# Two of three chunks of the last gate by way of DRAM, and the output projection two softmax steps sooner

## The chip, the cores and the metric

The kernel runs on one core of one Trainium2 chip. The metric is device time in microseconds (us), the median of several executions. TensorE (PE) multiplies, VectorE (DVE) and ScalarE (ACT) do elementwise work, GpSimd (POOL) does some too and issues DMAs, and SyncE (SP) only issues DMAs. The engines run side by side, each in a fixed order of instructions, and wait for one another by semaphores. A scheduler fixes each engine's order when the program is built.

## What is computed

Two layers of an encoder on 16 + 1024 = 1040 positions of width 1024, in float32. Each layer has a gated linear attention (GLA, 4 heads), a softmax attention with a forget-gate bias (FoX, 8 heads of 64), an output projection of both with a residual add, and a convolutional MLP. The part that matters here:

```python
xn = rms_norm(h, attn_norm[i])
gq, gk, gv, gr, glr, fq, fk, fv, ff = jnp.split(xn @ w_in[i], cuts, axis=-1)
...
o_gla = rms_norm(o_gla, gla_norm[i].reshape(GLA_HEADS, GLA_DV)).reshape(B, L, GLA_WIDTH)
o_gla = o_gla * jax.nn.silu(gr)
...
o_fox = forgetting_attention(fq.reshape(B, L, FOX_HEADS, FOX_DH),
                             fk.reshape(B, L, FOX_HEADS, FOX_DH),
                             fv.reshape(B, L, FOX_HEADS, FOX_DH), log_f).astype(h.dtype)
o_fox = rms_norm(o_fox, fox_norm[i].reshape(FOX_HEADS, FOX_DH)).reshape(B, L, FOX_WIDTH)
h = h + jnp.concatenate([o_gla, o_fox], axis=-1) @ w_out[i]
```

`silu(gr)`, with `gr` = four column blocks of 128 of the input projection, is "the gate" below: gate h belongs to GLA head h.

## The kernel before

Activations stand transposed: 128 features on the partitions, positions along the free axis, so a 1040-wide row is one of KD = 8 tiles. Float32 products are made of three fast matmuls (`mm3`, L249 to L255): each operand is split into a high and a low part (on ACT L378 the high, on DVE L379 the low), and the products high x high (L253), low-weight x high (L254) and high-weight x low (L255) are added up in PSUM.

The attention half of a layer is one function, `fox()` (L844). It walks through 72 softmax steps: 4 pairs of FoX heads with 18 steps each, a step being one head and one tile of 116 rows. A step has score matmuls on PE (L740, L741), a masked score with its maximum on DVE (L748), the exponential on ACT, transposes (L777) whose results DVE and ACT split (`PT`), and products with V (L795); a fold at the end of a row group (L808 to L842) brings the normalised head output, which is stored to DRAM (`mixd`). The last pair begins at step 54.

Between those matmuls PE gets filler: units of dense matmuls from a queue (`Work`, L131). One unit (`unit`, L262) is one chunk of columns of one 128-feature output tile: K matmul triples (8 for an input projection, 7 here for the output projection) and an evacuation. The list `starts` says at which steps the queue is emptied and refilled by `plan(p)`; within a stretch the units are spread evenly over its steps. Before, `starts` = 4, 22, 40, 58, 62, 80:

- from step 40, `plan(2)`: the products q, k, v of the last pair (9 units) and gate 2 (3 units)
- from step 58, `plan(3)`: gate 3 (3 units, chunks of 348, 348 and 344 columns, from the right), and the loads of `land[0]`, `[1]`, `[2]`, `[4]`, `[5]`, the GLA and FoX outputs that wait in DRAM (`mixd`)
- from step 62, `plan(4)`: the first four tiles of the output projection (12 units of 256, 384 and 400 columns, from the right)

`land` are the seven tiles from which the output projection is made; their order in each unit is `KORD` = 4, 5, 0, 1, 2, 3, 6. `land[3]` is gate 3's tile: the evacuation in `gr_products` (L685) writes there directly, while gates 0, 1 and 2 write to a scratch tile `gx` and from there to `mixd` in DRAM (L708, a DMA on POOL). One chunk of a gate has six operations on DVE (L693, L696, L700, then L703, L704, L706 behind the next step's scores, `later`) and three on ACT (L697 to L699). The slots of `land` are those of the second last pair, so they are free from step 58.

The first unit of the output projection carries a `feed` (L1040 to L1051): the splits of the seven land tiles, at most a few ahead of each matmul triple, and the residual loads.

## Time and profile before

| | |
|---|---|
| three runs | 2507.65, 2507.73, 2510.3 us |
| profiled execution | 2508.94 us, its span 2507.2 |
| mean granted clock of TensorE | 0.998 of full speed |
| instructions | 48346 |
| DMA traffic | 258.25 MB, 103 GB/s on average |

A span is the time from the first to the last instruction of one profiled execution. A row of the timeline reads: start, duration, engine, line, operation, output and inputs by name, size, and in brackets how long the engine had been idle and who released it. Windows give each engine's busy time in a stretch with its count, the clock granted to PE and the share of the DMA engines. Waits are totals, counts and the longest. Matmuls are pipelined: one that takes 0.32 by its own may start 0.16 after the one before it, so costs are read from start to start.

### The profile page before, as it was taken

The page shows a single profiled execution, that of the slowest core. Times are in us where ns is not written, and L with a number is a line of the kernel's source. Part 1 is how long each engine was busy: PE and PEld are TensorE (multiplying, and loading weights), DVE is VectorE, ACT ScalarE, POOL GpSimd, SP SyncE. Part 2 cuts the span into 40 slices and gives each one's busy share as a digit, 9 for nine tenths or more (in the row PEclk, how much of TensorE's full clock was granted, in tenths as well). Part 3 has the DMA queues.
Part 4 walks back from the last instruction along what each step waited for, and adds up shares of the span by engine and source line. Part 5 has one row for each costly group of instructions (what it writes and reads, how often), then busy time and mean ns, then how long its engine had stood idle before and what let it go on. Part 6 is the DMA issues. An engine that isn't in the chain of part 4 may idle for free.

```text
span 2507.2 us, 48346 instructions
## 1 busy us (share of the span) xinstructions
PE 2457.3 (98%) x19282; PEld 2410.2 (96%) x19282; DVE 1718.2 (69%) x3287; ACT 1272.3 (51%) x2548; POOL 403.2 (16%) x578
## 2 busy tenths in 40 slices
PE   8999999999999999999999999999999999999998
PEld 7999999899999999999999999998999999999997
DVE  7655676769877777853565666776797777787445
ACT  7345666556444445631343565674564444455312
POOL 4033433110000000100210334331100000001002
PEclk9999999999999999999999999999999999999999
DMA  3232134342322224763312233153332222257622
GB/s 123 71 89 75 54 88 129 111 149 72 115 81 81 77 77 139 198 170 110 105 54 70 75 86 87 44 164 109 127 96 98 76 81 81 78 165 177 199 60 78
DMA packets 115955, 258.25 MB, mean 103 GB/s; under 512 B 14496, under 2 KB 31040, under 8 KB 115728
## 3 DMA queue, kind: packets, MB, share of 16 engines
q1 hardware_dynamic: 92832, 181.74, 23.3%
q0 software_dynamic: 22176, 72.68, 10.3%
q8 instruction: 151, 2.47, 0.4%
q10 hardware_dynamic: 720, 0.74, 0.1%
q14 instruction: 76, 0.62, 0.1%
HBM read 174.50 MB, written 67.81 MB: 97 GB/s over the span
## 4 chain that ended last, share of the span: by engine, by line
PE 65%; issue 16%; DVE 10%; DMA 4%; ACT 4%; POOL 1%; SPq 0%; DVEq 0%; POOLq 0%; ACTq 0%
PE mm L253 7%; PE mm L255 7%; PE mm L254 7%; PE up L253 6%; PE up L255 6%; PE up L254 6%; PE down L253 5%; PE down L255 5%; PE down L254 5%; PE av L795 3%; PE tr L777 2%; PE wo L253 1%; PE wo L255 1%; PE wo L254 1%; DVE P L748 1%
## 5 line engine op out<-in xcount | busy, mean ns | idle before, releaser
L253 PE MATMUL up<-x,hi 128*128 128x260 f32 (+1 forms) x2464 | 697.2, 283 | 2.2 <-DVE hg L1322 1.4
L255 PE MATMUL up<-x,hi 128*128 128x260 f32 (+1 forms) x2464 | 695.4, 282 | 2.4 <-DVE x L1144 2.4
L254 PE MATMUL up<-x,lo 128*128 128x260 f32 (+1 forms) x2464 | 696.1, 283 | 0.0
L255 PEld LDWEIGHTS up<-x,hi 128*128 128x128 f32 x2464 | 465.7, 189 | 3.3 <-DVE x L1144 3.3
L253 PEld LDWEIGHTS up<-x,hi 128*128 128x128 f32 x2464 | 464.7, 189 | 3.1 <-DVE hg L1322 1.8
L254 PEld LDWEIGHTS up<-x,lo 128*128 128x128 f32 x2464 | 464.9, 189 | 0.1
L1120 DVE TENSOR_TENSOR lo<-raw,hi 128x512 fp32r<-128x512 f32 x364 | 247.9, 685 | 184.7 <-ACT hi L1119 177.0
L253 PE MATMUL mm<-xh,hi 128*128 128x348 f32 (+4 forms) x1056 | 360.5, 341 | 0.0
L255 PE MATMUL mm<-xl,hi 128*128 128x348 f32 (+4 forms) x1056 | 339.2, 321 | 0.0
L254 PE MATMUL mm<-xh,lo 128*128 128x348 f32 (+4 forms) x1056 | 338.3, 320 | 0.0
L1119 ACT CAST hi<-raw 128x512 fp32r<-128x512 f32 x364 | 224.5, 620 | 146.5 <-PE up L255 84.4
L253 PEld LDWEIGHTS mm<-xh,hi 128*128 128x128 f32 x1056 | 199.6, 189 | 3.0 <-issue 2.1
L254 PEld LDWEIGHTS mm<-xh,lo 128*128 128x128 f32 x1056 | 199.5, 189 | 0.3
L254 PE MATMUL down<-ah,lo 128*128 128x260 f32 (+1 forms) x704 | 198.1, 281 | 0.4 <-DVE lo L222 0.4
L255 PE MATMUL down<-al,hi 128*128 128x260 f32 (+1 forms) x704 | 198.4, 282 | 0.0
L255 PEld LDWEIGHTS mm<-xl,hi 128*128 128x128 f32 x1056 | 198.3, 188 | 0.0
L253 PE MATMUL down<-ah,hi 128*128 128x260 f32 (+1 forms) x704 | 197.9, 281 | 0.0
L379 DVE TENSOR_TENSOR PT<-tr,PT 116x464 fp32r<-116x464 f32 (+3 forms) x240 | 122.6, 515 | 70.3 <-ACT PT L378 68.4
L220 ACT CAST hi<-raw 128x512 fp32r<-128x512 f32 (+1 forms) x160 | 96.8, 607 | 122.3 <-PE down L255 96.0
L756 ACT ACTIVATE P<-P,m 116x924 f32<-116x924 f32 (+4 forms) x144 | 110.5, 768 | 73.0 <-DVE m L748 70.1
L1347 POOL DMA_DIRECT2D actd<-cv x44 | 23.5, 535 | 763.9 <-DVE cv L1346 758.0
L777 PE MATMUL tr<-ident,P 116*116 116x116 f32 x704 | 143.2, 266 | 2.5 <-DVE PT L379 1.3
(303 smaller groups left out, 5733.0 us busy)
## 6 DMA issues: line engine op xcount, KB each, us to landing
raw<-in_wm_dram SPq DMA_DIRECT2D x322, 256.0 KB, 2.8
raw<-in_wd_dram SPq DMA_DIRECT2D x64, 256.0 KB, 4.0
actd<-cv POOLq DMA_DIRECT2D x22, 520.0 KB, 2.9
actd<-cv POOLq DMA_DIRECT2D x22, 512.0 KB, 3.0
cb<-cd SPq DMA_DIRECT2D x16, 520.0 KB, 4.0
st<-actd SPq DMA_DIRECT2D x14, 520.0 KB, 4.7
st<-actd SPq DMA_DIRECT2D x14, 512.0 KB, 4.6
kA<-kA SPq DMA_DIRECT2D x24, 260.0 KB, 4.2
```

Source lines behind the costliest of these rows:

```text
L220: nc.scalar.copy(hi[:, :n, :], raw[:, :n, :])
L253: nc.tensor.matmul(ps, wh, xh[:, c0:c0 + n], start=first, stop=False, skip_group_check=more)
L254: nc.tensor.matmul(ps, wl, xh[:, c0:c0 + n], start=False, stop=False, skip_group_check=more)
L255: nc.tensor.matmul(ps, wh, xl[:, c0:c0 + n], start=False, stop=last, skip_group_check=more)
L379: nc.vector.tensor_tensor(out=lo, in0=src, in1=hi.bitcast(F32), op=ALU.subtract)
L748: self.scored = nc.vector.tensor_tensor_reduce(out=x, in0=S[:rows, :n], in1=cb[:rows, c0:k1], scale=1.0, scalar=(BIG if ci == 0 else m[:ro ...
L756: nc.scalar.activation(x, x, AF.Exp, scale=-1.0, bias=low, accum_out=(den if nch < 3 else d2[:rows, 0:1]))
L777: nc.tensor.transpose(tr[:w, j, :rows], P[:rows, o:o + w], id_)
L795: nc.tensor.matmul(av[:, a:width], w.rearrange("p a b -> p (a b)"), x, start=(t == 0 and i == 0), stop=(t == last and i == 1))
L1119: nc.scalar.copy(hi[:, :nk, :], src[:, :nk, :])
L1120: nc.vector.tensor_tensor(out=lo[:, :nk, :], in0=src[:, :nk, :], in1=hi[:, :nk, :].bitcast(F32), op=ALU.subtract)
L1347: nc.gpsimd.dma_start(self.actd[j][:, o0:T], uo)
```

## The change

`gr_products` gets a choice of chunks and of weights. Gate 3's chunks 2 and 1 (columns 692 to 1040 and 344 to 692) join `plan(2)`, that is, 14 units instead of 12 from step 40 to 58; they are stored to `mixd[3]` and read back in one DMA once gate 3's last chunk has been issued (`later`). `plan(3)` keeps chunk 0 alone (344 columns), with the weights that chunks 2 and 1 have loaded, and still writes to `land[3]`. `starts` gets 60 in place of 62. The other land tiles are loaded in two pieces each: columns 784 to 1040 on SP, the first 784 on POOL; `land[2]` is no longer held back.

```diff
--- before.py
+++ after.py
@@ -682,7 +682,7 @@
     def fox_free(self, q):
         self.slots.put(*q["qA"], *q["kA"], *q["kL"], *q["V"])

-    def gr_products(self, lyr, h, work, ap, pp, nm, dst=None):
+    def gr_products(self, lyr, h, work, ap, pp, nm, dst=None, chunks=CH_FOX, w=None):
         nc = self.nc

         def ev(ps, c0, n):
@@ -711,7 +711,7 @@
                 with self.tc.issue_after(self.scored.ins):
                     refine()
             self.later.append(behind)
-        self.add_tile(work, pp, self.wm[lyr, M_GR + h], nm["x"], CH_FOX if dst is None else CH_FOX[::-1], ev)
+        self.add_tile(work, pp, self.wm[lyr, M_GR + h], nm["x"], chunks, ev, w=w)


     @staticmethod
@@ -850,7 +850,7 @@
         steps = [(p, g, e, ti) for p in range(4) for g in range(5) for e in range(2)
                  for ti in reversed(range(len(groups[g])))]
         first = [steps.index((p, 0, 0, 1)) for p in range(4)]
-        starts = [f + 4 for f in first] + [first[3] + 8, len(steps) + 8]
+        starts = [f + 4 for f in first] + [first[3] + 6, len(steps) + 8]
         cbs, state, due = {}, {}, {}
         work, p_next = plan(-1), 0

@@ -1022,12 +1022,18 @@
                     if p < 3:
                         self.fox_products(lyr, p + 1, w, ap, pp, nm, qs[p + 1])
                         self.gr_products(lyr, p, w, ap, pp, nm)
+                        if p == 2:
+                            self.gr_products(lyr, 3, w, ap, pp, nm, chunks=CH_FOX[:0:-1])
+                            box["gate"] = w.boxes[-1]
                     elif p == 3:
                         land = box["land"] = [s.get(F32, f"h{k}") for k in range(KD - 1)]
-                        for k in (4, 5, 0, 1):
-                            nc.gpsimd.dma_start(land[k][:, :T], self.mixd[k][:])
-                        self.later.append(lambda: nc.gpsimd.dma_start(land[2][:, :T], self.mixd[2][:]))
-                        self.gr_products(lyr, 3, w, ap, pp, nm, land[3])
+                        c2, c3 = CH[2][0], CH_FOX[0][1]
+                        for k in (4, 5, 0, 1, 2):
+                            nc.sync.dma_start(land[k][:, c2:T], self.mixd[k][:, c2:T])
+                        for k in (4, 5, 0, 1, 2):
+                            nc.gpsimd.dma_start(land[k][:, :c2], self.mixd[k][:, :c2])
+                        self.later.append(lambda: nc.gpsimd.dma_start(land[3][:, c3:T], self.mixd[3][:, c3:T]))
+                        self.gr_products(lyr, 3, w, ap, pp, nm, land[3], CH_FOX[:1], box["gate"]["w"])
                     elif p == 4:
                         land = box["land"]
                         for c0, n in reversed(CH):
```

Where instructions move is shown at three places, all in layer 0.

VectorE up to the low split of gate 3's tile for the projection's first unit (`ml3` of 128x256); `ml4`, `ml5`, `ml6` are the same for the other tiles, `P` and `PT` belong to the softmax, and `P_6041` and `P_6038` are the first scores behind it. Before:

```order
L379 TENSOR_TENSOR ml5_5999<-h5_5668,mh5_5998 128x256
L693 TENSOR_TENSOR gx_5977<-mm_5899,r_149 128x344
L818 TENSOR_REDUCE fv_5943<-fo_5934 116x4
L696 TENSOR_SCALAR ge_5976<-gx_5977 128x344
L700 TENSOR_TENSOR gog_5974<-gx_5977,gog_5974 128x344
L222 TENSOR_TENSOR lo_6056<-raw_6053,hi_6055 128x512
L222 TENSOR_TENSOR lo_6062<-raw_6059,hi_6061 128x512
L379 TENSOR_TENSOR ml2_5993<-h2_5665,mh2_5992 128x256
L379 TENSOR_TENSOR ml3_5995<-h3_5666,mh3_5994 128x256
L748 ISA P_6041,m_6037<-S_6038,cb_5375 116x460
L379 TENSOR_TENSOR ml6_6001<-h6_5669,mh6_6000 128x256
```

And in the changed kernel:

```order
L379 TENSOR_TENSOR ml6_5915<-h6_5761,mh6_5914 128x256
L748 ISA P_5953,m_5949<-S_5950,cb_5448 116x460
L379 TENSOR_TENSOR ml4_5911<-h4_5759,mh4_5910 128x384
L748 ISA P_5953,m_5949<-S_5955,cb_5448,m_5949 116x348
L379 TENSOR_TENSOR ml5_5913<-h5_5760,mh5_5912 128x384
L379 TENSOR_TENSOR PT0_5940<-tr_5942,PT0_5940 116x4x116
L379 TENSOR_TENSOR ml6_5915<-h6_5761,mh6_5914 128x384
L379 TENSOR_TENSOR ml4_5911<-h4_5759,mh4_5910 128x400
L379 TENSOR_TENSOR ml5_5913<-h5_5760,mh5_5912 128x400
L379 TENSOR_TENSOR ml6_5915<-h6_5761,mh6_5914 128x400
L379 TENSOR_TENSOR ml3_5909<-h3_5758,mh3_5908 128x256
L748 ISA P_6038,m_6034<-S_6035,cb_5448 116x460
```

Before, a gate chunk, a fold and two weight splits stand ahead of `ml3`, and `ml6` behind it. In the changed kernel three tiles' splits of all columns stand ahead of it, `ml6` among them.

TensorE in the projection's first unit (`mm_6065` before, `mm_5977` in the changed kernel), from its fifth to its seventh operand and to the scores (`S`) of the next step. Before:

```order
L253 MATMUL mm_6065<-mh2_5992,hi_6007 128x256
L254 MATMUL mm_6065<-mh2_5992,lo_6008 128x256
L255 MATMUL mm_6065<-ml2_5993,hi_6007 128x256
L253 MATMUL mm_6065<-mh3_5994,hi_6007 128x256
L254 MATMUL mm_6065<-mh3_5994,lo_6008 128x256
L255 MATMUL mm_6065<-ml3_5995,hi_6007 128x256
L255 MATMUL mm_6065<-ml6_6001,hi_6013 128x256
L740 MATMUL S_6126<-kA0_4516,qA0_4514 116x460
```

In the changed kernel:

```order
L253 MATMUL mm_5977<-mh2_5906,hi_5921 128x256
L254 MATMUL mm_5977<-mh2_5906,lo_5922 128x256
L255 MATMUL mm_5977<-ml2_5907,hi_5921 128x256
L253 MATMUL mm_5977<-mh3_5908,hi_5921 128x256
L254 MATMUL mm_5977<-mh3_5908,lo_5922 128x256
L255 MATMUL mm_5977<-ml3_5909,hi_5921 128x256
L777 MATMUL tr_6027<-ident_61,P_5854 116x116
L740 MATMUL S_6035<-kA1_4517,qA1_4515 116x460
```

The scores `S_6126` belong to a later step than `S_6035`: the unit starts 2 steps of the softmax sooner, and from the start of step 54 to `ml3`'s matmul there are 239 matmuls where there were 317. The scores now come between operand 3 and operand 6.

GpSimd between the second last store of a FoX tile and the loads of `land[2]` (before) and `land[3]` (changed); `gx` is a gate's chunk, `h` the land tiles, `mixd` their places in DRAM, `in_hT0_dram` the residual. Before:

```order
L708 DMA mixd2_92<-gx_5559 128x348
L842 DMA mixd6_96<-fst_5807 128x112
L708 DMA mixd2_92<-gx_5655 128x348
L1034 DMA h6_5669<-mixd6_96 128x400
L1029 DMA h2_5665<-mixd2_92 128x1040
L913 TENSOR_TENSOR cb_5376<-cb_5376,mask_66 116x116
L1050 DMA h0_5663<-in_hT0_dram 128x256
```

In the changed kernel:

```order
L708 DMA mixd3_93<-gx_5651 128x348
L913 TENSOR_TENSOR cb_5447<-cb_5447,mask_66 116x116
L1056 DMA h0_5755<-in_hT0_dram 128x256
L1056 DMA h2_5757<-in_hT0_dram 128x400
L913 TENSOR_TENSOR cb_5447<-cb_5447,mask_66 116x116
L842 DMA mixd6_96<-fst_5867 128x112
L1040 DMA h6_5761<-mixd6_96 128x400
L708 DMA mixd3_93<-gx_5747 128x348
L1035 DMA h3_5758<-mixd3_93 128x696
L913 TENSOR_TENSOR cb_5448<-cb_5448,mask_66 116x116
```

What used to be gate 2's last store and `land[2]`'s load in whole is now gate 3's second chunk and 696 columns of `land[3]`; nine residual loads (rows 198 to 206 of this queue, the first and the last shown) now come ahead of it where they came behind.

## The prediction

> **What bounds the kernel now.** I read the page's busy shares first, then the stretch between the start of the last pair's softmax and the output projection as sums by window, then TensorE's waits there, then single instructions.
>
> ```profile
> PE 2457.3 (98%) x19282; PEld 2410.2 (96%) x19282; DVE 1718.2 (69%) x3287; ACT 1272.3 (51%) x2548; POOL 403.2 (16%) x578
> ```
>
> TensorE (PE) is busy 98% of the span. Whatever it has to multiply is the same after the change, so the change can only add or remove idle time of PE, of which there is 50 us in all. Where it lies is a question of stages, so here are windows of layer 0 (406 to 512), one before them, and layer 1's copy of the first:
>
> ```profile
> core 0: us, PE busy (x) PEld busy (x) DVE busy (x) ACT busy (x) POOL busy (x), PEclk, DMA share, GB/s
> 337.00:400.00 63.00, 62.84 (x455) 60.88 (x454) 41.45 (x126) 39.53 (x102) 26.04 (x36) 1.00 0.28 74
> 406.26:452.90 46.64, 44.69 (x318) 42.34 (x316) 40.00 (x124) 34.88 (x94) 13.96 (x25) 1.00 0.43 138
> 408.01:453.17 45.16, 43.21 (x309) 40.98 (x307) 40.00 (x125) 34.65 (x93) 13.96 (x25) 1.00 0.41 132
> 452.90:470.00 17.10, 13.57 (x88) 12.29 (x88) 16.03 (x44) 10.23 (x27) 6.63 (x13) 1.00 0.60 203
> 470.00:512.00 42.00, 41.10 (x283) 40.32 (x284) 25.09 (x79) 18.48 (x60) 1.72 (x4) 1.00 0.21 67
> 1645.25:1691.50 46.25, 44.48 (x317) 42.26 (x316) 40.28 (x124) 34.84 (x94) 14.19 (x25) 1.00 0.43 140
> ```
>
> Before 400 us and after 470 us VectorE (DVE) has a third of its time free. From 406.26 (step 54, the last pair's first scores) to 470 it has almost none: 40.00 of 45.16 us, then 16.03 of 17.10. Here both engines are nearly full, and PE is idle 1.95 and 3.53 us in the two windows, **5.5 us per layer**. Layer 1 is the same (1.77 in its first window). PE's waits name DVE for all of it:
>
> ```profile
> PE mm L255 <- DVE ml L379: 2.5, 2, 1.7
> PE av L795 <- DVE PT L379: 2.0, 3, 1.2
> PE S L740 <- DVE m L748: 0.6, 1, 0.6
> PE tr L834 <- DVE ff L823: 0.3, 1, 0.3
> ```
>
> Half of it is the projection's first unit waiting for low parts (ml) that DVE splits off:
>
> ```profile
> 452.82 0.39 PE L255 MATMUL mm<-ml,hi 128*128 128x256 f32 x1 [0.81 <-DVE ml L379]
> 453.04 0.28 PE L253 MATMUL mm<-mh,hi 128*128 128x256 f32 x1
> ...
> 455.57 0.39 PE L255 MATMUL mm<-ml,hi 128*128 128x256 f32 x1 [1.72 <-DVE ml L379]
> ```
>
> So the question to put to the change is not how much work it removes (none), but which work of PE and which of DVE it moves into or out of this full stretch. I measure both up to one point that both programs have: k=3's low matmul of the projection's first unit, which reads `ml3`, 256 columns.
>
> **PE's side.** Before, PE's last scores of step 54 start at 406.26 and it does about 44.7 us of work to that point (the window row). The order of rows, counted from step 54 to that matmul, loses these: 36 gate matmuls (1.5 units, now ahead of step 54), and softmax work of the last two steps, now behind it: two pairs of 460-wide score matmuls, a 232 and a 116 pair, 13 transposes, 14 products with V, 7 small ones. Their spacings:
>
> ```profile
> 406.26 0.45 PE L740 MATMUL S<-kA,qA 128*116 128x460 f32 x1
> 406.55 0.37 PE L741 MATMUL S<-kL,qA 128*116 128x460 f32 x1
> 406.75 0.37 PE L740 MATMUL S<-kA,qA 128*116 128x464 f32 x1
> ...
> 427.53 0.32 PE L253 MATMUL mm<-xh,hi 128*128 128x348 f32 x1
> 427.69 0.32 PE L254 MATMUL mm<-xh,lo 128*128 128x348 f32 x1
> ...
> 451.28 0.49 PE L777 MATMUL tr<-ident,P 116*116 116x116 f32 x3
> 451.53 0.36 PE L253 MATMUL mm<-mh,hi 128*128 128x256 f32 x1
> ```
>
> Gate: 36 x 0.16 = 5.8 us. Scores: 2 x 0.49, and about 0.4 for the two narrow pairs; transposes 13 x 0.08 = 1.1; V products 14 x 0.12 (256-wide matmuls stand 0.12 apart) = 1.6; the rest 0.4: together 4.5. PE's work to the point becomes 44.7 - 10.3 = **34.4 us**. The projection's own matmuls to that point are the same in both.
>
> **DVE's side.** From its first score of step 54 (408.01, waiting for a bias row, 1.75 us behind PE) to the `ml3` split it worked 40.00 us. The order shows what changes in that interval. Added: one 256-wide, five 384-wide and six 400-wide splits of other tiles, which the scheduler now puts ahead of `ml3`, since those tiles are loaded earlier and `ml3` is late. Removed: a P of 460 and of 232, PT of 464, 348 and 232, the first three steps of one gate chunk, a fold, and four V splits.
>
> ```profile
> 408.01 0.64 DVE L748 CUSTOM_DVE_ANT_0 P<-S,cb 116x460 f32<-116x460 f32 x1 [0.79 <-DMA cb<-cd]
> ...
> 443.85 0.62 DVE L748 CUSTOM_DVE_ANT_0 P<-S,cb 116x460 f32<-116x460 f32 x1
> 444.40 0.08 DVE L748 DVE_READ_ACCUMULATOR2_ANT m<- 116x1 f32 x1
> 444.40 0.55 DVE L379 TENSOR_TENSOR ml<-h,mh 128x384 fp32r<-128x384 f32 x1
> 444.87 0.45 DVE L748 CUSTOM_DVE_ANT_0 P<-S,cb,m 116x232 f32<-116x232 f32 x1
> ...
> 446.67 0.63 DVE L379 TENSOR_TENSOR PT<-tr,PT 116x464 fp32r<-116x464 f32 x1
> 447.22 0.51 DVE L704 SCALAR_TENSOR_TENSOR gy<-ge,gy 128x348 f32<-128x348 f32 x1
> ...
> 449.57 0.51 DVE L693 TENSOR_TENSOR gx<-mm,r 128x344 f32<-128x344 f32 x1
> 450.00 0.41 DVE L818 TENSOR_REDUCE fv<-fo 116x4 f32<-116x256 f32 x1
> 450.33 0.33 DVE L696 TENSOR_SCALAR ge<-gx 128x344 f32<-128x344 f32 x1
> ```
>
> By start-to-start times, a 384 split costs 0.47, a P of 460 0.55, a PT of 464 0.55, a gate step about 0.43 (L696 0.25). Added: 0.34 + 11 x 0.48 = 5.6. Removed: P 0.55 + 0.38, PT 0.55 + 0.43 + 0.31, gate 1.1, fold 0.9, V some 0.7: 4.9. DVE's work becomes **40.7 us**. The gate's DVE work does leave the stretch in part, but its place is taken by splits that stood behind the point before.
>
> **The sum.** Before, the two sides met: PE 44.7 of work, DVE 1.75 + 40.0 plus waits. After, PE reaches `ml3` 10.3 us of work sooner and DVE no sooner. PE's idle time up to the point is 1.75 + 40.7 + w - 34.4 = 8.05 + w, where w is what DVE itself stands still. In 408.01:453.17 it stood still 5.16 us, mostly because PE was then the later one; w lies between 0 and 5.2. I take 1.8, nearest to what is left when PE is no longer late: a wait for ScalarE in a gate chunk, and about 1 us for k=3's way through DRAM. That way is new, and its rows are these:
>
> ```profile
> 437.16 0.54 POOL L708 DMA_DIRECT2D mixd<-gx  x1 [0.49 <-DVE ge L696]
> 440.60 0.54 POOL L1029 DMA_DIRECT2D h<-mixd  x1 [1.56 <-DMA mixd<-gx]
> ...
> mixd<-gx POOLq DMA_DIRECT2D x1, 174.0 KB, 2.6
> h<-mixd POOLq DMA_DIRECT2D x1, 520.0 KB, 3.8
> ...
> L703 DVE SCALAR_TENSOR_TENSOR ge<-ge,gy 128x348 f32<-128x348 f32 x4 | 2.1, 516 | 0.9 <-ACT gy L699 0.9
> ```
>
> A store of a gate chunk lands 2.6 us after its issue, a load of 520 KB 3.8; the new load has 356 KB, so I estimate 3.2. With two issues and ScalarE's split it is some 7 us from the gate's last product to the `ml3` split, and DVE's order has about 6.7 us of other work in between. Behind the waiting load on POOL stand a mask and residual loads, which nobody needs soon; behind `ml3` on DVE stand the PT and P of the next steps, so a late load stops the softmax as well, and PE with it. The second bound, all of the 7 us uncovered, I do not reach, since the work between does not depend on it.
>
> So PE is idle 9.85 us up to the point, and about 0.3 after it (it then has two softmax steps more to work on than before, while DVE is done with most splits). Against 5.5 before: **+4.65 us per layer**. I estimate that its largest piece, at `ml3`, has 3 to 5 us: the order puts five splits in one run right ahead of PE's goal there (4 x 0.48 + 0.34 = 2.3 us), and k=3's late arrival and PT's turn come on top. The rest are waits for PT and scores. What a long wait does to PE's clock the trace shows in one place:
>
> ```profile
> 2361.95 0.58 PE L253 MATMUL down<-x,hi 128*128 128x256 f32 x1 [2.02 <-ACT dg L1501]
> ...
> 2358.43:2361.84 3.41, 1.50 (x13) 1.29 (x11) 0.40 (x1) 1.48 (x3) 0.00 (x0) 1.00 0.96 358
> 2361.84:2365.25 3.41, 3.31 (x15) 3.31 (x16) 3.29 (x5) 3.41 (x5) 0.00 (x0) 0.50 1.01 401
> ```
>
> After a wait of 2.02 us the granted clock was 0.50 for 3.41 us, in which PE got through 15 matmuls where 0.12 us spacing would have given 28: 1.6 us lost. I take 1.3 per layer, since part of that window is waiting anyway. The bounds are 0 and 1.6 per window hit. [...]
>
> The other edits cost nothing on the path. The split of the five tile loads into columns moves 10 loads of 128 and 392 KB to two queues; the order has them done long before their splits, and DVE's outside work has room. The two gate chunks moved to steps 40 to 58 bring 2 x 2.4 us of DVE work to a place with 21 us free in 63 (first window row); without that room they would delay the softmax by as much. Reusing the gate's weights saves nothing that PE waits for.
>
> Per layer 4.65 + 1.3 = 5.95, twice 11.9. The profiled execution took 2508.94 (span 2507.2), so 2520.8; it lies 1.2 above the median of the runs, 2507.73, so **2519.6 us**.
>
> **The rivals.** (A) The gate's DVE work leaves the full stretch and the four waits vanish. For it: 4.8 us of work leaves per layer, and the waits are 5.5. Against it: the order puts 5.6 us of splits in its place. It would give up to 2 x 4 us: 2500. It decides if DVE's work to `ml3` falls below about 34 - 1.75 us, which needs the splits of 384 and 400 columns not to hold it up. (B) No net change: the waits only move from `ml6` and PT to `ml3`, because PE runs ahead by as much as DVE catches up earlier, with DVE's start 1.75 us sooner: 2508, give or take 4. For it: totals are the same. Against it: DVE has no slack from 408 to 453 to catch up in. (C) k=3's way through DRAM is far later than I think (POOL has nine residual loads of some 0.55 us issue ahead of it, and 1.6 MB to share the DMA with): each late microsecond is one of PE, up to 3 per layer: 2526, and one more half-clock window each would bring 2529. (D) The change doesn't do what it says: the scheduler keeps the projection's start where it was. The order of after rules it out, since the first projection matmul stands ahead of two more steps.
>
> **How the numbers follow.** Forecast with w from 0 to 3.5 and clock from 0 to 1.6: 0.57; C 0.20; B 0.14; A 0.09. Range: with w = 0 and no clock 2.85 per layer, 2513.4; B's centre lies below, so I reach down to 2508, which leaves out A and half of B (0.16), and up to 2529. A measurement of this kernel tells 0.2% (5 us) from no change. Faster by that: A, 0.08. Within it: most of B and the forecast's lowest corner, 0.16. Slower: 0.76.
>
> **What would show it.** In the profile after: DVE near 95% from step 54 to `ml3` in both layers; PE idle near 10 us there, with one wait of 3 to 5 us for `ml` on L379 as its last piece; a clock of 0.50 for one window behind it; PE's waits for `ml6` gone. A median below 2508, or PE's idle time at `ml3` below 2 us, would show the account of DVE's work wrong; idle time at a `tr` or `S` that waits for a DMA would mean C.

## The result and the profile after

| | before | changed |
|---|---|---|
| median | 2509.14 us (5 runs, 2507.65 to 2510.3) | 2521.79 us (5 runs, 2517.63 to 2524.62) |
| ratio | 1 | 1.0054, 95% interval 1.0044 to 1.0065 |
| profiled span | 2507.2 us | 2520.0 us |

The forecast was 2519.6 us, slower than before. The first rows of the page of the changed kernel, to be read beside those of before:

```profile
span 2520.0 us, 48400 instructions
PE 2464.0 (98%) x19282; PEld 2416.2 (96%) x19282; DVE 1722.4 (68%) x3287; ACT 1273.8 (51%) x2548; POOL 408.0 (16%) x584
```

PE has the same 19282 matmuls, and yet it is busy 6.7 us longer: by the trace's clock records its clock was at 0.50 for 27.4 us of the span, against 8.8 before. The rest of the 12.8 us that the span has grown, 6.1, is idle time.

Where it lies shows when each trace is cut at rows that all kernels have: the 73rd score matmul of a layer (step 41, just behind the start of the filler with the moved chunks) and the first matmul of the MLP's up-projection. From one to the other, worked out from their start times:

| stretch | before | changed |
|---|---|---|
| layer 0, step 41 to the MLP | 214.6 us | 221.9 (+7.3) |
| layer 1, step 41 to the MLP | 214.2 | 219.5 (+5.3) |
| all else | 2078.4 | 2078.6 |

The same two stretches as windows (span, then PE's busy time; PEclk stands behind the five engines), the two layers of before and then the two of the changed kernel:

```profile
349.62:564.22 214.60, 208.05 (x1527) 202.15 (x1526) 148.87 (x403) 127.06 (x321) 55.86 (x92) 1.00 0.38 119
1588.63:1802.82 214.19, 207.76 (x1527) 201.95 (x1526) 148.94 (x403) 126.75 (x321) 56.16 (x92) 1.00 0.38 119
351.16:573.08 221.92, 212.54 (x1524) 206.07 (x1523) 150.89 (x402) 127.45 (x321) 57.89 (x94) 0.97 0.38 118
1597.02:1816.50 219.48, 208.09 (x1524) 202.42 (x1523) 150.25 (x402) 127.00 (x321) 57.97 (x94) 0.98 0.39 119
```

In layer 0 PE is busy 4.5 us longer and idle 2.8 longer (9.38 against 6.55), in layer 1 busy 0.3 and idle 5.0 longer (11.39 against 6.43). Together that is 7.8 us of idle time, where 2 x 4.65 = 9.3 were forecast, and 4.8 of busy time, where the clock term had 2 x 1.3 = 2.6. The other 1.9 us of busy time lie outside the two stretches, where idle time fell by 1.7.

PE's waits in layer 0 from 400 to 500 us, in the changed kernel (total, count, longest):

```profile
PE mm L253 <- ACT mh L378: 5.0, 1, 5.0
PE tr L834 <- DVE PT L379: 2.0, 1, 2.0
PE tr L777 <- DVE m L748: 0.5, 1, 0.5
PE av L795 <- DVE PT L379: 0.4, 1, 0.4
```

The four rows of before have given way to two large single waits. The timeline has them at the end of step 59 and at k=3 of the projection's first unit:

```profile
442.96 0.29 PE L834 MATMUL tr<-ident,ff 112*128 112x112 f32 x1 [1.99 <-DVE PT L379]
...
459.15 0.58 PE L253 MATMUL mm<-mh,hi 128*128 128x256 f32 x1 [5.05 <-ACT mh L378]
459.53 0.41 PE L254 MATMUL mm<-mh,lo 128*128 128x256 f32 x1
```

The place of the second was forecast, its releaser was not: PE waits for the high part (`mh`, ScalarE), so the tile itself is late, not VectorE's low part. In layer 1 that wait has 6.89 us. The windows from step 54 to k=3 in both layers, and three windows behind the two waits of layer 0:

```profile
core 0: us, PE busy (x) PEld busy (x) DVE busy (x) ACT busy (x) POOL busy (x), PEclk, DMA share, GB/s
412.88:459.25 46.37, 37.79 (x240) 34.38 (x239) 40.48 (x117) 32.89 (x84) 17.60 (x33) 0.91 0.56 177
444.60:448.01 3.41, 2.97 (x12) 2.26 (x11) 3.41 (x10) 3.18 (x9) 1.51 (x3) 0.50 0.78 247
448.01:451.40 3.39, 3.39 (x16) 3.05 (x15) 3.39 (x10) 1.98 (x5) 0.00 (x0) 0.51 0.73 241
459.25:462.65 3.40, 3.40 (x15) 3.16 (x16) 2.52 (x8) 1.35 (x5) 1.12 (x3) 0.50 0.97 350
1658.70:1704.20 45.50, 34.85 (x240) 31.89 (x239) 40.18 (x117) 32.87 (x84) 17.65 (x33) 0.96 0.58 177
```

The first row is the account of the prediction: VectorE 40.48 us of work, PE 37.79 at a mean clock of 0.91, which is about 34.4 at full clock. The three rows below it show what a wait costs beyond its own length: by the trace's clock records the clock is halved from 444.5 to 451.4, behind the wait of 1.99 us, and from 458.2 to 465.0, from within the wait of 5.05 on. Why the tile is late is in GpSimd's timeline:

```profile
446.39 0.55 POOL L842 DMA_DIRECT2D mixd<-fst  x1
451.75 0.55 POOL L1040 DMA_DIRECT2D h<-mixd  x1 [4.81 <-DMA mixd<-fst]
452.29 0.54 POOL L708 DMA_DIRECT2D mixd<-gx  x1
455.41 0.54 POOL L1035 DMA_DIRECT2D h<-mixd  x1 [2.57 <-DMA mixd<-gx]
```

and in the list of DMA issues from 446 to 456 us (KB each, us to landing):

```profile
h<-mixd POOLq DMA_DIRECT2D x1, 348.0 KB, 3.3
...
mixd<-fst POOLq DMA_DIRECT2D x1, 56.0 KB, 5.1
```

Gate 3's store (L708) stands behind a load of `land[6]` (L1040), which waits 4.81 us for a store of 56 KB to land. That store took 5.1 us, against 1.8 for the same store in layer 0 of before; the share of the DMA engines is 0.78 and 0.73 there (rows above). Only behind all this comes `land[3]`'s load.

### The profile page after: what moved, and what is told of

It reads as the page before. It is cut to its first block, busy times and chain, and to the rows that moved or that the text cites. A ratio compares the mean times of both kernels' runs of the same rounds, so it can differ in the third digit from the quotient of the medians.

```text
span 2520.0 us, 48400 instructions
## 1 busy us (share of the span) xinstructions
PE 2464.0 (98%) x19282; PEld 2416.2 (96%) x19282; DVE 1722.4 (68%) x3287; ACT 1273.8 (51%) x2548; POOL 408.0 (16%) x584
## 3 DMA queue, kind: packets, MB, share of 16 engines
q0 software_dynamic: 21952, 72.79, 10.3%
## 4 chain that ended last, share of the span: by engine, by line
PE 67%; issue 18%; DVE 8%; ACT 3%; DMA 3%; POOL 1%; SPq 0%; DVEq 0%; POOLq 0%; ACTq 0%
PE mm L253 8%; PE mm L254 8%; PE mm L255 8%; PE up L253 5%; PE up L254 5%; PE up L255 5%; PE down L253 4%; PE down L254 4%; PE down L255 4%; PE av L795 3%; PE tr L777 2%; PE wo L253 1%; PE wo L255 1%; PE wo L254 1%; PE S L741 1%
## 5 line engine op out<-in xcount | busy, mean ns | idle before, releaser
L1108 DVE TENSOR_TENSOR raw<-raw,raw 128x512 f32<-128x512 f32 x198 | 129.6, 687 | 19.5 <-DMA raw<-in_wd_dram 15.1
```

The lines of the kernel that those rows point to most:

```text
L1108: nc.vector.tensor_tensor(out=q[out][:, :nk, :], in0=q[a][:, :nk, :], in1=q[b][:, :nk, :], op=op)
```

## The experiments

Three theories; their letters are not those of the prediction's rivals. **A**, the prediction's: VectorE's work in the stretch sets the time, and the splits ahead of `ml3` are part of it. **B**: the way of `land[3]` through DRAM alone. **C**, which I formed after the first two sets of runs: the moved matmuls leave steps 58 to 60 short of filler, PE then waits some 2 us in one piece, and the halved clock costs as much as the waits. The table has all runs; the two columns on the right are the growth of the stretch from step 41 to the MLP against before, layer 0 and layer 1, from the profiled run. They rest on one execution each, which can lie some 2.6 us off the run's median (2512.65 against 2515.28 in e14), so differences of about 1 us between two runs are not shown.

| run | median us | ratio to before (95%) | layer 0 | layer 1 |
|---|---|---|---|---|
| the change | 2521.79 | 1.0054 (1.0044 to 1.0065) | +7.3 | +5.3 |
| e1 land[3] read back in two pieces | 2518.64 | 1.0040 (1.0028 to 1.0052) | +4.7 | +4.9 |
| e2 land[6] loaded by SP | 2517.76 | 1.0037 (1.0024 to 1.0049) | +4.8 | +5.4 |
| e3 start 60 alone | 2509.01 | 1.0002 (0.9993 to 1.0011) | +0.6 | +1.3 |
| e4 gate moved, start 62 | 2525.23 | 1.0067 (1.0055 to 1.0080) | +7.4 | +7.6 |
| e5 early flush | 2518.70 | 1.0045 (1.0032 to 1.0057) | +4.7 | +4.0 |
| e8 chunk 1 without DRAM | 2519.15 | 1.0046 (1.0034 to 1.0059) | +2.4 | +4.7 |
| e10 wide splits held back | 2521.29 | 1.0054 (1.0040 to 1.0068) | +2.9 | +3.3 |
| e11 splits on GpSimd | 2523.59 | 1.0063 (1.0050 to 1.0075) | +4.6 | +5.2 |
| e12 useless filler | 2514.86 | 1.0026 (1.0015 to 1.0036) | +0.4 | +1.6 |
| e13 one chunk moved | 2515.23 | 1.0023 (1.0013 to 1.0034) | +1.5 | +0.9 |
| e14 one chunk, paced | 2515.28 | 1.0024 (1.0015 to 1.0034) | +1.0 | +0.8 |
| e15 start 60, paced | 2510.49 | 1.0012 (1.0003 to 1.0021) | +0.1 | +1.0 |

In their profiles the runs from e8 to e14 carry a loss of 2.8 to 4.0 us that lies outside the attention: a wait in layer 0's MLP that grew from 1.07 us before (0.51 in the changed kernel) to 3.2 or more. The matmul behind it takes 0.58 us in e8, against 0.39 before, as the same matmul did at a clock of 0.50 behind the 2.02 us wait that the prediction shows. In e8:

```profile
1126.86 0.58 PE L253 MATMUL down<-x,hi 128*128 128x260 f32 x1 [3.38 <-ACT dg L1509]
```

Its cause was not tried; ahead of it ScalarE waits for a load (`st<-actd`), 5.25 us in e14 against 2.55 in the changed kernel. So their medians overstate what they lose in the stretch, and the two columns on the right are the ones to read.

All runs but e3 and e15 also have the other edits of the change, the loads of the land tiles in two pieces and `land[2]` without delay. These were not tried alone.

### e1: land[3] read back in two pieces

```diff
-self.later.append(lambda: nc.gpsimd.dma_start(land[3][:, c3:T], self.mixd[3][:, c3:T]))
+c4 = CH_FOX[1][0] + CH_FOX[1][1]
+nc.sync.dma_start(land[3][:, c4:T], self.mixd[3][:, c4:T])
+self.later.append(lambda: nc.gpsimd.dma_start(land[3][:, c3:c4], self.mixd[3][:, c3:c4]))
```

> The changed kernel, but land[3] is read back in two pieces: columns 692 to 1040 on SP as soon as plan(3) begins, columns 344 to 692 later on POOL as before. The projection's first unit then waits for nothing that is still on its way through DRAM; all arithmetic stays. Theory A (VectorE's work in the full stretch sets the time, a late land[3] only adds VectorE's own standing still): PE's single wait for mh of k=3 (5.05 us in layer 0, 6.89 in layer 1) goes, but 2 to 3 us per layer come back as waits for PT, ml or mh of tile 6: 2515 to 2518 us. Theory B (the way of land[3] through DRAM, queued on POOL behind the wait for the FoX tile's store, is the whole cause): all of it goes, and the half-clock windows behind it: 2506 to 2510 us.

2518.64 us. The wait at k=3 is gone, but waits of 1.01 and 2.53 us at the fold of the pair's second row group (`fo`, for PT and for `avs`) have come in its place in layer 0, 1.11 and 2.60 in layer 1, and in layer 0 the granted clock is 0.72 on average from 454 to 462 us and 0.86 from 462 to 470. 3 us of 12.65 come back, 0.6 less than A's range has at least, and B is out.

### e2: land[6] loaded by SP

```diff
-nc.gpsimd.dma_start(land[6][:, c0:c0 + n], self.mixd[6][:, c0:c0 + n])
+nc.sync.dma_start(land[6][:, c0:c0 + n], self.mixd[6][:, c0:c0 + n])
```

> The changed kernel, but the three loads of land[6] are issued by SP instead of POOL, so POOL no longer stands 4.8 us waiting for the FoX tile's store to land before it can issue gate 3's store. land[3] should arrive about 3.7 us sooner. Theory A: VectorE is then itself late by 1 to 2 us, so the wait for k=3 shrinks from 5 to 7 us to 1.5 to 3: 2514 to 2518 us. Theory B: the wait shrinks by the whole 3.7 us per layer, with some of the clock: 2511 to 2514 us. If POOL's wait had nothing to do with it: 2521 us.

2517.76 us, as A had it. The wait at k=3 fell from 5.05 and 6.89 to 2.96 and 4.65: so GpSimd's wait for the small store was worth 2.1 and 2.2 us at that place. The 4.65 of layer 1 is more than the 1.5 to 3 us that A had for it.

### e3: the earlier start alone, in the kernel before

```diff
-starts = [f + 4 for f in first] + [first[3] + 8, len(steps) + 8]
+starts = [f + 4 for f in first] + [first[3] + 6, len(steps) + 8]
```

> The kernel before, with 60 in place of 62 in starts and nothing else: gate 3 keeps its three units, now in two steps, and still writes to land[3] without DRAM. Theory A: VectorE has the three gate chunks and the splits in two steps less, PE's work to the first unit's k=3 shrinks by about 4.5 us and VectorE's by less, so slower than before: 2511 to 2516 us. Theory B: nothing goes through DRAM that did not before, so not slower: 2506 to 2510 us.

2509.01 us, ratio 1.0002: nothing clear of noise, where A had 2 to 7 us; that is inside B's range. The window from step 54 to just ahead of k=3's low matmul, the sixth of the unit, in this run (PE's row 406.26:452.90 in the prediction ends as far ahead of it):

```profile
406.11:448.34 42.23, 39.91 (x277) 38.02 (x277) 36.40 (x111) 31.55 (x84) 13.63 (x25) 1.00 0.49 159
```

VectorE's work to the point is 36.40 us, 3.6 less than before, and PE's 39.91, 4.8 less: starting earlier moves two steps' work of both engines behind the point, and here no wide splits take the place of VectorE's. VectorE's falls by less than PE's, as A said, but the time did not follow. The longest wait is 1.85 us, and the clock stays at 1.00.

### e4: the moved gate alone (the change with the old start)

```diff
-starts = [f + 4 for f in first] + [first[3] + 6, len(steps) + 8]
+starts = [f + 4 for f in first] + [first[3] + 8, len(steps) + 8]
```

> The changed kernel with 62 in starts: gate 3's two chunks go through DRAM, but the projection begins where it did before. Theory A: PE's work to k=3 is 5.8 us less than before (the moved gate matmuls), VectorE's 2 to 4 us less: 1 to 2 us per layer slower than before, 2510 to 2514 us. Theory B: land[3] has two softmax steps (some 9 us) more to arrive, which covers the 5 to 7 us: 2507 to 2510 us.

2525.23 us, worse than the whole change; both theories had too little. So all of the loss comes with the moved chunks and the loads changed with them, and the earlier start gives some of it back. `land[3]` is just as late (PE waits 4.34 us at k=3), although the projection begins later:

```profile
463.59 0.39 PE L253 MATMUL mm<-mh,hi 128*128 128x256 f32 x1 [4.34 <-ACT mh L378]
```

The reason can be read in the code: chunk 1's last operations and its store are put off (`later`) until the next unit of filler is done, and that is the one unit left in `plan(3)`, which is spread over four steps here, over two in the changed kernel. The next run takes the delay away.

### e5: the postponed work at step 58

```diff
-self.later.append(lambda: nc.gpsimd.dma_start(land[3][:, c3:T], self.mixd[3][:, c3:T]))
+self.flush()
+nc.gpsimd.dma_start(land[3][:, c3:T], self.mixd[3][:, c3:T])
```

> The changed kernel, but the postponed part of gate 3's chunk 1 (three VectorE operations and its store) and the read-back of land[3] are issued when plan(3) begins, at step 58, and not after gate 3's last unit two steps later. The way through DRAM stays. Theory A (two causes: land[3] late, 5 to 7 us at k=3; and PE without gate filler running ahead of VectorE in steps 56 to 58, the 2.0 us wait for PT with a halved clock behind it): the first goes, the second stays, 2513 to 2517 us. Theory B (land[3]'s lateness alone): 2507 to 2511 us. If the way through DRAM is late however early it begins: 2519 or more.

2518.70 us, above A's range. The wait for `mh` is gone; the wait for PT at the end of step 59 has grown from 2.0 to 2.7 us:

```profile
PE tr L834 <- DVE PT L379: 2.7, 1, 2.7
PE fo L808 <- DVE PT L379: 1.8, 2, 1.5
PE tr L777 <- DVE m L748: 1.2, 1, 1.2
PE tr L777 <- DVE PT L379: 1.0, 1, 1.0
```

### e8: chunk 1 straight into land[3]

```diff
-to = x if dst is None else dst[:, c0:c0 + n]
+to = x if dst is None else dst(c0)[:, c0:c0 + n] if callable(dst) and dst(c0) is not None else x if callable(dst) else dst[:, c0:c0 + n]
...
-self.gr_products(lyr, 3, w, ap, pp, nm, chunks=CH_FOX[:0:-1])
+self.gr_products(lyr, 3, w, ap, pp, nm, lambda c0: box["land"][3] if "land" in box else None, CH_FOX[:0:-1])
...
+c4 = CH_FOX[1][0] + CH_FOX[1][1]
-self.later.append(lambda: nc.gpsimd.dma_start(land[3][:, c3:T], self.mixd[3][:, c3:T]))
+nc.sync.dma_start(land[3][:, c4:T], self.mixd[3][:, c4:T])
+self.flush()
```

> As the run with the early flush, but gate 3's chunk 1 is written by VectorE straight into land[3], which exists by then, and only chunk 2 goes through DRAM, read back on SP at step 58: nothing of land[3] is then on its way when the projection begins. All arithmetic is the same. Theory A: PE's wait for k=3 is under 1 us, the wait for PT near 2 us in step 57 and the half clock behind it stay: 2512 to 2516 us. Theory B: 2506 to 2510 us.

2519.15 us, above both ranges; 4.0 us of it are the MLP's, without which it would lie in A's. In the stretch 5.5 of the 12.6 us have gone and 7.1 stay, with nothing of `land[3]` on its way any more. What stays is waits for VectorE (PE's waits, layer 0) and the clock (a window behind the longest of them):

```profile
PE tr L834 <- DVE PT L379: 2.7, 1, 2.7
PE av L795 <- DVE PT L379: 1.4, 3, 0.6
PE tr L777 <- DVE PT L379: 0.9, 1, 0.9
```

```profile
442.80:449.60 6.80, 6.37 (x27) 5.68 (x26) 6.80 (x18) 6.53 (x16) 2.11 (x5) 0.50 0.81 254
```

PE's idle time in the two stretches is 14.4 us, against 13.0 before, and its busy time 421.5 against 415.8: most of the 7.1 us is the clock. Behind the 2.7 us it is halved for 6.8 us, and in layer 1 for 10.2. This is where theory C came from.

### e10: the wide splits held back, on top of e8

```diff
-            nc.vector.tensor_tensor(out=lo, in0=src, in1=hi.bitcast(F32), op=ALU.subtract)
+            return nc.vector.tensor_tensor(out=lo, in0=src, in1=hi.bitcast(F32), op=ALU.subtract)
...
 def one(k):
-    self.split(mix[k][0][:, c0:c0 + n], mix[k][1][:, c0:c0 + n], land[k][:, c0:c0 + n])
+    with tc.issue_after(box["low"].ins) if j < 2 else nullcontext():
+        low = self.split(mix[k][0][:, c0:c0 + n], mix[k][1][:, c0:c0 + n], land[k][:, c0:c0 + n])
+    if j == 2:
+        box["low"] = low
```

> The run with chunk 1 straight into land[3], and on VectorE the low splits of 384 and 400 columns are queued behind the seven low splits of 256 columns that the first projection unit needs (issue order alone, no wait). Before k=3's split stand then about 5 us less of VectorE work. Theory A, with my account of VectorE's work: the PT wait in step 57 does not shrink much if no splits stand ahead of it, but the waits in steps 58 to 60 do, 1 to 3 us per layer less than without the hold: 2508 to 2513 us. Rival: the order of splits does not matter, since PE waits for PT and the scores in any case: the same time as without the hold, within 2 us.

2521.29 us in all, 2.1 more than e8; in the stretch 0.9 us less (6.2 against 7.1), which is not clear of noise. So A's gain is not there, and the rival holds to about its 2 us. The wait in step 59 falls from 2.73 to 1.99 and 2.04 us, VectorE itself now waits 1.09 us for ScalarE ahead of the PT there, the clock behind the wait is 0.54 on average from 443 to 446 us in layer 0, and a wait of 2.25 and 2.05 us stands further on. The order of the splits, on which the prediction's term of 5.6 us rests, is not what the time hangs on.

### e11: six low splits on GpSimd, on top of e8

```diff
-self.split(mix[k][0][:, c0:c0 + n], mix[k][1][:, c0:c0 + n], land[k][:, c0:c0 + n])
+hi, lo, x = mix[k][0][:, c0:c0 + n], mix[k][1][:, c0:c0 + n], land[k][:, c0:c0 + n]
+if k in (0, 1):
+    nc.scalar.copy(hi, x)
+    nc.gpsimd.tensor_tensor(out=lo, in0=x, in1=hi.bitcast(F32), op=ALU.subtract)
+else:
+    self.split(hi, lo, x)
```

> The run with chunk 1 straight into land[3], but the low splits of land[0] and land[1] (three chunks each) are computed by GpSimd instead of VectorE. VectorE has 2.6 us less to do per layer in the full stretch. If VectorE's amount of work sets the time there: 2 to 3 us per layer less than without it, 2508 to 2512 us. Rival: GpSimd is too slow or too far behind in its queue (its masks of 116 by 116 take about 0.5 us, a split of 400 columns would be 1.5 us or more), so the projection waits for ml0 or ml1, or the masks come late for the scores: not faster than without it, 2512 to 2520 us.

2523.59 us: slower by 4.4 than e8, on the rival's side and beyond its range, though not for the rival's reason. A GpSimd split takes 0.73 to 1.04 us, less than feared. But VectorE's busy time rose by 7.2 us (1721.7 in e8, 1728.9 here) with 12 instructions fewer. What happens is in the section on the hardware. A is not tested by this run.

### e12: a unit of filler that nobody reads, on top of e8

```diff
+def extra():
+    ps = pp.tile([128, 512], F32, tag="mm", name="mm")
+    for k in range(KD):
+        self.mm3(ps[:, :c3], box["gate"]["w"][k], nm["x"][k], 0, c3, k == 0, k == KD - 1)
+        yield 3 * mm_us(c3)
+w.add(extra(), KD * 3 * mm_us(c3))
 self.gr_products(lyr, 3, w, ap, pp, nm, land[3], CH_FOX[:1], box["gate"]["w"])
```

> The run with chunk 1 straight into land[3], plus one unit of 24 matmuls per layer whose product nobody reads, as extra filler for PE in steps 58 to 60 (gate 3's chunk 0 computed a first time into a PSUM tile that is dropped). PE's work grows by 2 x 3.8 = 7.7 us and nothing else changes. Theory C (PE short of filler in steps 58 to 60 runs ahead of VectorE, waits 2.7 us for PT in one piece, and the clock is halved for two windows behind it, 10.8 us of busy time in all): the wait in step 59 falls below 1.5 us, the clock stays full, and the kernel is no slower or even faster in spite of the extra work: 2510 to 2517 us. Rival (the clock is not set off by that wait; what counts is VectorE's work): the extra work fills 2 x 2.7 us of waiting and the rest comes on top: 2520 to 2524 us.

2514.86 us: 48 matmuls more, 7.7 us of work, and 4.3 us less time than e8. The waits of layer 0 and the window that ran at 0.50 in e8:

```profile
PE tr L777 <- DVE PT L379: 1.4, 1, 1.4
PE fo L808 <- ACT avs L798: 0.5, 1, 0.5
```

```profile
442.80:446.20 3.40, 3.40 (x27) 3.30 (x25) 3.40 (x9) 3.40 (x12) 2.68 (x6) 1.00 0.75 196
```

The wait in step 59 is gone and the clock is 1.00. The clock is still halved for 3.4 us further on in layer 0, behind the 1.4 us:

```profile
455.25:458.67 3.42, 3.42 (x15) 3.35 (x14) 3.25 (x11) 1.93 (x6) 0.63 (x1) 0.50 0.99 380
```

In the stretch only 2.0 of e8's 7.1 us stay. PE is idle 8.4 us where it was 14.4, and busy 422.4, of which 7.7 are the added unit's: without them that is about the 415.8 of before. No data arrives sooner and VectorE has no less to do. C is shown, then, for 5.1 of the 12.6 us; 5.5 went with the DRAM way and the delays on it (e8), and 2.0 stay, which are not taken apart further; the added unit's own work is among what PE has to do here.

### e13 and e14: one chunk moved instead of two

```diff
-self.gr_products(lyr, 3, w, ap, pp, nm, chunks=CH_FOX[:0:-1])
+self.gr_products(lyr, 3, w, ap, pp, nm, chunks=CH_FOX[2:])
...
-self.later.append(lambda: nc.gpsimd.dma_start(land[3][:, c3:T], self.mixd[3][:, c3:T]))
-self.gr_products(lyr, 3, w, ap, pp, nm, land[3], CH_FOX[:1], box["gate"]["w"])
+c4 = CH_FOX[1][0] + CH_FOX[1][1]
+self.later.append(lambda: nc.sync.dma_start(land[3][:, c4:T], self.mixd[3][:, c4:T]))
+self.gr_products(lyr, 3, w, ap, pp, nm, land[3], CH_FOX[1::-1], box["gate"]["w"])
```

And in e14 besides, at the softmax's exponential and in the function that issues one split:

```diff
-nc.scalar.activation(x, x, AF.Exp, scale=-1.0, bias=low, accum_out=(den if nch < 3 else d2[:rows, 0:1]))
+self.expd = nc.scalar.activation(x, x, AF.Exp, scale=-1.0, bias=low, accum_out=(den if nch < 3 else d2[:rows, 0:1]))
...
-self.split(mix[k][0][:, c0:c0 + n], mix[k][1][:, c0:c0 + n], land[k][:, c0:c0 + n])
+with tc.issue_after(self.scored.ins) if j < 2 else nullcontext(), \
+        tc.issue_after(self.expd.ins) if j < 2 else nullcontext():
+    self.split(mix[k][0][:, c0:c0 + n], mix[k][1][:, c0:c0 + n], land[k][:, c0:c0 + n])
```

> The changed kernel with one of gate 3's chunks moved instead of two: chunk 2 alone joins plan(2) and goes through DRAM, chunks 1 and 0 stay in plan(3), in two steps, and write straight into land[3]. PE has twice the filler in steps 58 to 60. Theory C: no wait reaches 2 us, the clock stays full, the time is that of the kernel before within 0.2%: 2505 to 2512 us. Rival (any gate chunk moved ahead of step 54 costs its cover, 3.9 us of PE per layer): 2513 to 2517 us.

> The run with one chunk moved, and the splits of 384 and 400 columns (both halves, ScalarE's and VectorE's) are queued behind the scores and the exponential of the softmax step in which the program has them, so that they no longer stand in one row of eight on VectorE (4.18 us) and of five on ScalarE ahead of step 60's PT and avs. Theory C: the 2.11 us wait for avs falls below 1.8 us in both layers, the clock stays full, and the time is that of the kernel before or a little less: 2504 to 2510 us. Rival (the late splits only move the wait to the second unit's ml, equally long): 2513 to 2517 us.

2515.23 and 2515.28 us, both above C's ranges and inside the rivals': e13's by about the MLP's 3.3 us, e14's by 2 us more than the MLP's 3.1. C's other signs are missed in part as well, since the clock was halved in layer 0 of both (0.50 from 456.4 to 459.8 us in e13). The mechanism of e13's rival is not borne out, since it has 3.9 us per layer and the stretch lost 1.5 and 0.9. In the stretch e13 loses 2.4 us (1.5 + 0.9) and e14 1.8, against 12.6 for two chunks. e13 has no wait of note in step 59, but one of 2.12 us at the next place where splits stand in one run on VectorE, eight in 4.18 us (VectorE's timeline, then PE's waits):

```profile
449.94 4.18 DVE L379 TENSOR_TENSOR ml<-h,mh 128x256 fp32r<-128x256 f32 x8
```

```profile
PE fo L808 <- ACT avs L798: 2.1, 1, 2.1
```

In e14 that wait falls to 0.2 us in layer 0, below the 1.8 expected. The longest wait of the stretch is now 1.31 us, for VectorE's PT, but the clock is halved behind it all the same in layer 0, for 3.4 us. A gain over e13 is not shown: the medians are equal, and 0.6 us in the stretch is within the noise.

### e15: the earlier start with the pacing

The same lines of pacing on e3.

> The kernel before with 60 in place of 62 in starts, no gate chunk moved, and the same pacing of the splits of 384 and 400 columns. It had no clock loss, so only PE's idle time can shrink, from 7 us per layer: by theory C a gain of 1 to 3 us per layer against the kernel before, 2502 to 2507 us. Rival: VectorE's amount of work sets the idle time whatever the order: 2507 to 2510 us.

2510.49 us, ratio 1.0012 (1.0003 to 1.0021), where up to 6 us of gain were expected: its longest wait in the stretch is 1.33 us, and the clock shows no loss (0.998 on average over the profiled run, as before), but the stretch takes no less than before. That is nearer the rival, and slightly above its range. No kernel of these beats the one before.

## Why the prediction was right

**Time and sign**: +12.65 us measured, +11.9 forecast, inside the range; the mechanism was right in part only. The growth per layer (7.3 and 5.3, plus 0.5 and 0.3 ahead of step 41) lies around the 5.95 that were summed up.

**The two engines' work.** PE about 34.4 us to k=3 in layer 0, forecast 34.4, and 34.85 in layer 1; VectorE 40.48 and 40.18, forecast 40.7. (The windows end some 0.4 to 0.5 us ahead of k=3's low matmul, before as well as after.) Counting the order's rows and pricing them from start to start was good to a fraction of a microsecond.

**Idle time to the point.** Forecast 9.85; measured 8.58 in layer 0 (46.37 - 37.79) and 10.65 in layer 1 (45.50 - 34.85). Of its parts, VectorE began 0.95 us behind PE and not 1.75, and w was 4.9 (46.37 - 0.95 - 40.48) and not 1.8, almost the upper bound. Most of it is one wait for ScalarE's PT, which stood behind a split of 400 columns that waited for the load of `land[6]`:

```profile
455.99 0.64 DVE L379 TENSOR_TENSOR PT<-tr,PT 116x464 fp32r<-116x464 f32 x1 [3.41 <-ACT PT L378]
...
454.61 0.53 ACT L378 CAST mh<-h 128x400 fp32r<-128x400 f32 x1 [3.65 <-DMA h<-mixd]
```

**The signs that it named.** PE's idle time near 10 us (8.58 and 10.65) and the end of the waits for `ml6` came. VectorE near 95% did not: it was busy 87 and 88% of the two windows. The last piece was longer than 3 to 5 us (5.05 and 6.89), and PE waited there for ScalarE's `mh` and not for VectorE's `ml`.

**What failed in it** is the step "PE reaches `ml3` 10.3 us of work sooner and DVE no sooner", read as a cause. The single runs split it. The 4.5 us that came from the earlier start cost nothing clear of noise (e3), where VectorE is relieved of 3.6 us alongside. The 5.8 us of gate matmuls that left the stretch do cost, but not because splits stand ahead of `ml3` (e10 queues them behind it and wins nothing clear of noise). Moving them sends the tile through DRAM, and it leaves steps 58 to 60 with one unit of filler where there were three in four steps, so that PE waits in step 59 (1.99 us in the change, 2.7 without the DRAM way). A useless unit in that place wins back 5.1 of 7.1 us (e12).

**Rival C, `land[3]` late through DRAM**, which I gave 0.20 as an extra, is true as a part: 5.5 of the 12.6 us went in e8, which also takes the delay in the code away. Its price was about right (up to 3 us per layer), its mechanism half: the nine residual loads ahead of the store do not hold it up by their issue time, the 4.81 us wait for `land[6]`'s store does, and the code's own postponement (e4, e5).

**The clock term was mis-sized.** 1.3 us per layer forecast; PE's busy time in the stretch grew by 4.5 us in layer 0 and 0.3 in layer 1. I counted one window of 3.41 us at half clock for each layer; layer 0 has 13.7 us of it (6.8 for each wait), layer 1 6.8, through the first 3.4 of which PE waited. The idle term was mis-sized the other way: 7.8 us more, where 9.3 were forecast. The sum came out since both errors cancel, which is luck.

**Rival A**: the gate's VectorE work did leave, and two of the four waits (for `ml`) are gone from the list of after, but nothing was won. **Rival B** did not happen with the change; e3 is the kernel for which it holds.

The length of a wait alone does not tell whether half clock follows: behind 1.88 us in e4 the clock was 0.51 from 443.4 to 446.8 us, and the same wait at the end of step 59 of e5 had half clock behind it in layer 0 (2.73 us) and none in layer 1 (2.72).

## What to carry to other kernels

Filler that moves ahead of a stretch in which two engines are nearly full must be priced by what it covered there, and not by the work that it takes from the other engine: look for the step that is left with too little of it. A wait of about 2 us on TensorE may cost more than twice its length: behind the 1.99 us of the changed kernel PE was busy for 6.36 us at a clock of 0.50 (2.97 and 3.39, from 444.60 to 451.40), which by my estimate lost another 3.2 us. It did not do so everywhere: behind 2.73 us in layer 0 of e5 the clock was 0.50, behind 2.72 in layer 1 it stayed at 1.00. A single wait of that length was not needed either: in the stretch of layer 0 none of e12 and e14 was longer than 1.4 us, and 3.4 us at half clock followed in each all the same. And before sending a tile through DRAM, read the queue that issues the store: a load ahead of it that waits for a small store delays both (by 4.81 us in layer 0 here).

## What the runs showed of the hardware

**The clock.** Waits of PE from 1.88 to 2.73 us were followed by half clock for 3.4, 6.8 or more us in some places (1.88 us in e4: 0.51 from 443.4 to 446.8; 1.99 in the changed kernel: 0.50 from 444.5 to 451.4; 2.73 in e8: 0.50 from 442.8 to 449.6) and not in others (2.72 in layer 1 of e5); the waits of 1.85 (twice in e3) and 1.82 (before, layer 1) were not. The same wait has 2.73 us in layer 0 of e5 and 2.72 in layer 1, here the second on PE's timeline, then a window that holds most of the wait and the next one, in layer 0 and in layer 1:

```profile
1686.75 0.29 PE L834 MATMUL tr<-ident,ff 112*128 112x112 f32 x1 [2.72 <-DVE PT L379]
```

```profile
439.45:442.87 3.42, 1.10 (x9) 0.81 (x7) 3.42 (x9) 3.42 (x11) 2.81 (x6) 1.00 0.39 118
442.87:446.28 3.41, 3.00 (x12) 2.81 (x12) 3.41 (x11) 2.35 (x7) 2.60 (x6) 0.50 0.88 258
1685.32:1688.73 3.41, 1.88 (x12) 1.59 (x12) 3.41 (x10) 3.39 (x10) 3.16 (x7) 1.00 0.81 249
1688.73:1692.15 3.42, 2.09 (x16) 1.82 (x16) 2.44 (x9) 1.13 (x3) 1.21 (x3) 1.00 0.91 276
```

In layer 0 the first window has 1.10 us of PE's work, and the clock is 0.50 in the 3.41 us behind it. In layer 1 the first has 1.88, the second 2.09, and the clock stays at 1.00. What decides whether half clock follows a wait is not shown.

**VectorE's operations beside GpSimd's splits.** In e11, an operation on 112 x 2 numbers took VectorE 2.17 us, and a gate product 2.44, each while GpSimd worked on splits; in e8 the same two take 0.16 and 0.52. VectorE's rows come first, GpSimd's behind the dots, all of e11:

```profile
434.78 2.17 DVE L325 SCALAR_TENSOR_TENSOR fy<-fa,fy 112x2 f32<-112x2 f32 x1
440.01 2.44 DVE L706 SCALAR_TENSOR_TENSOR h<-gy,gog 128x348 f32<-128x348 f32 x1
...
435.21 1.71 POOL L1057 TENSOR_TENSOR ml<-h,mh 128x256 fp32r<-128x256 f32 x2
440.34 1.72 POOL L1057 TENSOR_TENSOR ml<-h,mh 128x400 fp32r<-128x400 f32 x2
```

VectorE's operation ends when GpSimd's pair of splits does, to within 0.4 us (436.95 and 436.92; 442.45 and 442.06). Which of the two came first, and what held VectorE up, the rows do not show: VectorE's rows start 0.43 and 0.33 us ahead of GpSimd's, whose times are rough.
